# Moving one low-part subtraction to GpSimd and the gate's activation ahead of it, at the turn from gate/up to down in the wide experts

## The chip, the core and the metric

One core of a Trainium2 chip runs the whole block: TensorE (PE, with its weight loads PEld), VectorE (DVE), ScalarE (ACT), GpSimd (POOL) and SyncE (SP), which issues most weight loads. The metric is the device time of one launch in microseconds (us).

## The reference, cut to what matters

The block is a gated MLP mixer and a gated delta net, then a mixture of 32 experts, four for each of 512 tokens. The change lies in the expert's middle:

```python
gu = xb @ w_gu[e] + b_gu[e]
gate = jnp.minimum(gu[:, :D_FF], SWIGLU_LIMIT)
up = jnp.clip(gu[:, D_FF:], -SWIGLU_LIMIT, SWIGLU_LIMIT)
act = gate * jax.nn.sigmoid(SWIGLU_ALPHA * gate) * (up + 1)
return (act @ w_down[e] + b_down[e]) * wt[:, None]
```

`w_gu` is 1024 x 2048 and `w_down` 1024 x 1024 for each expert, all in float32.

## The kernel before, in words

Experts are sorted by their number of tokens and each sits at a fixed place p, 0 to 31, in the program; `CAPS[RANKS[p]]` is the number of rows that the place can hold. Eight places hold 128 rows or more and are called wide here: p = 3, 9, 17 and 29 hold 128; p = 5, 13, 21 and 25 hold 192 or 160, that is a `Wide` unit of 128 rows and a second `Unit` of 64 or 32. The other 24 places are narrow and use plain float32 matmuls.

A wide place computes with float32r matmuls in three passes: weights and activations are split into a high part (`hi`, a copy rounded to float32r) and a low part (`lo`, the difference). `split_w` makes both for one 128 x 1024 piece of weights: the high part is a copy on ACT (L1410, `whi`), the low part a subtraction on DVE (L1411, `wlo`). Three pairs of buffers go round (`N_PAIRS = 3`). A place has 16 such pieces for gate/up and 8 for down, and the pair of the second down piece was last used by the gate/up piece next to last.

`run(p, ...)` is one place: the gate/up matmuls over eight chunks of weights, then the turn, then the down matmuls over eight pieces f. In the turn of a wide place each half c (512 columns) goes through `swiglu`: on ACT a relu and a sigmoid of the gate (L1423, L1424), on DVE the clipped up part `u` (L1425), the product with the gate `r` (L1426) and `u = (u + 1) * r` (L1427), where both inputs are SBUF tiles of `f16` (in the trace they are called f). PE transposes each half (L1549), ACT copies it as the high part `ath` (L1551) and DVE subtracts for the low part `atl` (L1552). `between` transposes the next place's rows on PE, and `behind` modulates them on ACT and DVE.

From here on every engine's order is that of the code (a manual schedule). The weights pass through a ring of 14 chunks of 1 MB: SP loads a chunk ahead as soon as PE, or the split, has read the slot. On GpSimd's queue only gathers (L1302) and the adding scatters of finished rows (L1764) run in this stage; in the first 320 us, GpSimd has made low parts of other weights (L158) with the same kind of instruction.

Of the kernel before, what the change touches and what calls it, by code (L numbers as in the profile page):

```python
# [6 lines left out]
F32 = mybir.dt.float32  # L7
# [5 lines left out]
OP = mybir.AluOpType  # L13
# [43 lines left out]
def hybrid_block(tc, x, c, w_ada, b_ada, norm1_w, w_in, gm_vnorm_w, gm_w_spatial, gm_b_spatial,  # L57
# [3 lines left out]
    V, S, G, T = nc.vector, nc.scalar, nc.gpsimd, nc.tensor  # L61
# [110 lines left out]
    ready = []  # L172
# [11 lines left out]
    def take():  # L184
        ahead(3)
        n_used[0] += 1
        return ready[n_used[0] - 1]
# [66 lines left out]
    for f in range(3):  # L254
        w = take()
# [42 lines left out]
    for n in range(5):  # L298
        V.tensor_scalar(ta[:, 0, :], ta[:, 2, :], n, 1, op0=OP.logical_shift_right,
                        op1=OP.bitwise_or)  # L300
# [383 lines left out]
    for f in range(3):  # L684
        w = take()
# [81 lines left out]
    for n in range(4):  # L767
        p1s = []
        for gs in halves:
            p1 = bank([P, 8, 32])  # L770
            p1s.append(p1)
            for c8 in range(8):
                for q in range(4):
                    r = slice(q * 32, q * 32 + 32)
# [5 lines left out]
        for gs in halves:  # L780
            p2 = bank([P, 8, 32])
            p2s.append(p2)
            for c8 in range(8):
                for q in range(4):
                    r = slice(q * 32, q * 32 + 32)
# [37 lines left out]
    for g in range(4):  # L823
        gs = slice(g * 4, g * 4 + 4)
        kk = bank([P, 4, 2, CH])
        for c4 in range(4):
            ch, hp = divmod(g * 4 + c4, 2)
            for hb in range(2):
                r = slice(hb * 64, hb * 64 + 64)
# [23 lines left out]
    for g in range(2):  # L853
        for hb in range(2):
            r = slice(hb * 64, hb * 64 + 64)
# [142 lines left out]
    w = [take() for _ in range(4)]  # L998
# [45 lines left out]
    def load_chunk(i):  # L1044

        p, j = divmod(i, 12)
        if p < NE:
            load_part(ring[i % N_RING], bass.ds(ids[p], 1) if p else slice(0, 1), j)

    def load_id(p):  # L1050
        if p >= NE or not p:
            return
        ids[p] = nc.values_load(eids[0:1, p:p + 1], engines=[mybir.EngineType.SP], min_val=0, max_val=NE - 1,
                                skip_runtime_bounds_check_because="a permutation of the experts")

    op = ExitStack()
# [117 lines left out]
    both = range(2)  # L1174
# [83 lines left out]
    act_tiles = [f16[:, 2 + i // 2, (i % 2) * 512:(i % 2) * 512 + 512] for i in range(4)]  # L1258
# [142 lines left out]
                part.turn()  # L1401
                part.modulate()

    def split_w(w):

        i = n_split[0] % N_PAIRS
        n_split[0] += 1
        hi = xp.tile([P, D], F32R, name="whi", tag=f"x2_{2 * i}") if i < 2 else mp.tile([P, D], F32R, name="whi", bufs=1)
        lo = xp.tile([P, D], F32R, name="wlo", tag=f"x2_{2 * i + 1}") if i < 2 else mp.tile([P, D], F32R, name="wlo", bufs=1)
        S.activation(hi, w, AF.Copy)  # L1410
        V.tensor_tensor(lo, w, hi.bitcast(F32), op=OP.subtract)  # L1411
        return hi, lo

    n_split = [0]
# [2 lines left out]

        return ((h[0], w[0]), (h[1], w[0]), (h[0], w[1]))

    def swiglu(gate, up, r, u):  # L1420

        n = gate.shape[0]
        S.activation(r, gate, AF.Relu, scale=-1.0, bias=sevens[0:n, 0:1])  # L1423
        S.activation(r, r, AF.Sigmoid, scale=-1.702, bias=sevens[0:n, 1:2])  # L1424
        V.tensor_scalar(u, up, 7.0, -7.0, op0=OP.min, op1=OP.max)  # L1425
        V.scalar_tensor_tensor(r, gate, 7.0, r, op0=OP.min, op1=OP.mult)  # L1426
        V.scalar_tensor_tensor(u, u, 1.0, r, op0=OP.add, op1=OP.mult)  # L1427
        return u

    class Unit:  # L1430
# [43 lines left out]
        def act(self):  # L1474
            i = (0, 1) if not self.second else (0, 2) if self.part.first else (2, 3)
            r, u = (act_tiles[j][:, 0:self.w] for j in i)
            self.a = swiglu(self.gate, self.up, r, u)
# [40 lines left out]
    class Wide:  # L1518


        n, w, ng, off, second, banks = P, D, 1, 0, False, 5
# [17 lines left out]
                    mm(self.gu[c * 2 + q], l[:, k, :], r[:, q * 512:q * 512 + 512], False, k == KC - 1 and i == 2)  # L1539

        def act(self):
            self.a = [swiglu(self.gu[c], self.gu[2 + c], act_tiles[2 * c], act_tiles[2 * c + 1]) for c in both]

        def turn(self):
            self.at, self.al = (mp.tile([P, KC, P], F32R, name=nm, bufs=1) for nm in ("ath", "atl"))
# [200 lines left out]
    def last_rows(u):  # L1746

        y_last, junk, rest, same, factor, nf_u = (last_tiles[nm] for nm in ("y_last", "junk", "rest", "same", "factor", "nf_u"))
        y, s_ = y_last[:, 0:u.w], ssn[:, NT:NT + 1]
        V.tensor_tensor(y, u.dn, factor[:, 0:u.w], op=OP.mult)  # L1750
        V.tensor_tensor(y, y, rest[:, 0:u.w], op=OP.add)  # L1751
        V.scalar_tensor_tensor(junk[:, 0:u.w], y, 1.0, y, op0=OP.mult, op1=OP.mult, accum_out=s_)  # L1752
        ps = psT2.tile([P, 512], F32, name="t")[:, 0:1]
        mm(ps, same, s_)
        norm(s_, ps)
        V.scalar_tensor_tensor(y, y, s_, nf_u[:, 0:u.w], op0=OP.mult, op1=OP.mult)  # L1756
        G.indirect_dma_start(out=u.rows(out[0]), out_offset=bass.IndirectOffsetOnAxis(ap=u.idx, axis=0), in_=y,  # L1757
                             in_offset=None, bounds_check=SEQ * D // u.w - 1, oob_is_err=False)

    def add_rows(u):  # L1760

        y = mp.tile([P, 512 if u.second else D], F32, name="yx" if u.second else "yo", bufs=1)[:, 0:u.w]
        u.weighted(y)
        G.indirect_dma_start(out=u.rows(acc), out_offset=bass.IndirectOffsetOnAxis(ap=u.idx, axis=0),  # L1764
                             in_=y, in_offset=None, compute_op=OP.add,
                             bounds_check=SEQ * D // u.w - 1, oob_is_err=False)

    def run(p, side, between, behind):

        units = place[p].units
        w = [ring[(p * 12 + j) % N_RING] for j in range(12)]
        load_id(p + 3)
        for u in units:
            u.gu_start()
        split = place[p].split
        for k in range(KC):
            if split:
                for c in both:  # L1780
                    units[0].gu_parts(k, c, split_w(w[k][:, c * D:(c + 1) * D]))
            for u in units[split:]:
                u.gu_chunk(k, w[k])
            load_chunk(p * 12 + k + N_RING)
            side(k)

        def source(f):
            return w[KC + f // 2][:, (f % 2) * D:(f % 2) * D + D]

        ready = [split_w(source(0))] if split else []  # L1790
        for u in units:
            u.act()
        between()
        room = sum(u.banks for u in units) + len(units) < 6
        for u in units if room else ():
            u.down_start()
        for u in units:
            u.turn()
        for u in () if room else units:
            u.down_start()  # L1800
        if split:
            ready += [split_w(source(1)), split_w(source(2))]
        for f in range(KC):
            behind(f)
            if split:
                units[0].down_parts(f, ready.pop(0) if ready else split_w(source(f)))
            for u in units[split:]:
                u.down_chunk(f, source(f))
            if f % 2:
                load_chunk(p * 12 + KC + f // 2 + N_RING)  # L1810
        for u in units:
            last_rows(u) if p == NE - 1 else add_rows(u)
# [11 lines left out]
    def side(p):  # L1824
        def at(k):
            if k == 0:
                hots(p + 2)
            elif k == 1 and not late(p):
                find(p + 2)
            elif k == 2 and not late(p):  # L1830
                spread(p + 2)

        return at

    def between(p):
        def at():
            if p == 0:
                for _ in steps:
                    pass
                spread(2)  # L1840
            place[p + 1].turn()
            if p and late(p):
                find(p + 2)

        return at

    def behind(p):
        def at(f):
            if f == 0:
                place[p + 1].parts[0].modulate()  # L1850
            elif f == 4:
                place[p + 1].more_turn()
                if p + 2 < NE:
                    if p and late(p):
                        spread(p + 2)
                    place[p + 2].gather()

        return at

    run(0, side_0, between(0), behind(0))  # L1860
    for p in range(1, NE - 1):
        run(p, side(p), between(p), behind(p))
    run(NE - 1, lambda k: early(k, place[NE - 1].units[0]), lambda: None, early_norms)


# [80 lines left out]
```

## Time and profile before

| | us |
|---|---|
| median of three runs (lowest, highest) | 1528.15 (1523.21, 1534.48) |
| profiled execution | 1526.17 |
| its span, first to last instruction | 1524.4 |
| PE busy | 1401.4 (92%) |
| DVE busy | 694.7 (46%) |
| ACT busy | 475.7 (31%) |
| GpSimd busy | 237.0 (16%) |

Matmuls are pipelined, so a busy PE need not be at its peak, and busy time at a granted clock of one half counts like any other. Shares are averages: the expert stage lies from about 364 us to 1507 us.

### The profile page before, as it was taken

The page shows a single profiled execution, that of the slowest core. Times are in us where ns is not written, and L with a number is a line of the kernel's source. Part 1 is how long each engine was busy: PE and PEld are TensorE (multiplying, and loading weights), DVE is VectorE, ACT ScalarE, POOL GpSimd, SP SyncE. Part 2 cuts the span into 40 slices and gives each one's busy share as a digit, 9 for nine tenths or more (in the row PEclk, how much of TensorE's full clock was granted, in tenths as well). Part 3 has the DMA queues.
Part 4 walks back from the last instruction along what each step waited for, and adds up shares of the span by engine and source line. Part 5 has one row for each costly group of instructions (what it writes and reads, how often), then busy time and mean ns, then how long its engine had stood idle before and what let it go on. Part 6 is the DMA issues. An engine that isn't in the chain of part 4 may idle for free. (4 is left out here: it accounts for less than half of the span.)

```text
span 1524.4 us, 23439 instructions
## 1 busy us (share of the span) xinstructions
PE 1401.4 (92%) x9161; PEld 737.2 (48%) x9161; DVE 694.7 (46%) x1352; ACT 475.7 (31%) x735; POOL 237.0 (16%) x218
## 2 busy tenths in 40 slices
PE   4898999998899999999999999999999999999982
PEld 3555897775337454246334523642454235424621
DVE  4674628984229453147115512831462146214713
ACT  4343332321127242135015411711351135113501
POOL 2243433530011100110010011000101010101010
PEclk9999999998999999999999999999999999999995
DMA  9566331168699996999999699999978997899973
GB/s 326 180 240 212 99 117 47 59 249 354 240 404 410 401 398 205 407 396 407 395 407 408 230 370 406 404 391 409 399 309 317 410 387 264 308 411 396 390 295 119
DMA packets 113698, 479.35 MB, mean 314 GB/s; under 512 B 15172, under 2 KB 28649, under 8 KB 80811
## 3 DMA queue, kind: packets, MB, share of 16 engines
q1 hardware_dynamic: 98176, 454.10, 76.2%
q0 software_dynamic: 10096, 18.87, 5.1%
q10 hardware_dynamic: 5306, 4.80, 1.0%
q8 instruction: 74, 1.21, 0.3%
q14 instruction: 46, 0.37, 0.1%
HBM read 466.21 MB, written 17.96 MB: 318 GB/s over the span
## 5 line engine op out<-in xcount | busy, mean ns | idle before, releaser
L71 PE MATMUL gu<-ring,h 128*64 128x512 f32 (+1 forms) x1984 | 381.1, 599 | 0.0
L1411 DVE TENSOR_TENSOR wlo<-ring,whi 128x1024 fp32r<-128x1024 f32 x192 | 229.2, 1222 | 48.8 <-ACT whi L1410 47.8
L71 PE MATMUL gu<-ring,at 128*32 128x256 f32 (+1 forms) x1536 | 237.4, 508 | 13.9 <-ACT at L1485 13.9
L1410 ACT ACTIVATE whi<-ring 128x1024 fp32r<-128x1024 f32 x192 | 200.7, 1060 | 115.0 <-PE gu L71 92.1
L71 PEld LDWEIGHTS gu<-ring,h 128*64 128x64 f32 (+1 forms) x1984 | 104.8, 128 | 245.0 <-issue 232.0
L1423 ACT ACTIVATE f<-gu,sevens 128x512 f32<-128x512 f32 (+1 forms) x51 | 32.1, 630 | 529.7 <-PE gu L71 527.5
L1425 DVE TENSOR_SCALAR f<-gu 128x512 f32<-128x512 f32 (+1 forms) x51 | 31.7, 622 | 298.1 <-PE gu L71 280.5
L71 PEld LDWEIGHTS gu<-ring,at 128*32 128x32 f32 (+1 forms) x1536 | 64.7, 125 | 164.7 <-issue 129.7
L1302 POOL DMA_INDIRECT f<-xnd,idx x35 | 36.0, 1028 | 537.4 <-PE gu L1483 277.4
L1764 POOL DMA_INDIRECT acc<-yo,idx x31 | 55.9, 1802 | 401.5 <-DVE yo L1505 238.0
L158 POOL TENSOR_TENSOR wlo<-w,whi 128x1024 fp32r<-128x1024 f32 x32 | 80.8, 2530 | 138.2 <-ACT whi L157 135.9
L71 PE MATMUL gu<-whi,hh 128*128 128x512 f32 x256 | 84.1, 410 | 0.0
L71 PE MATMUL gu<-wlo,hh 128*128 128x512 f32 x256 | 80.8, 397 | 0.8 <-DVE wlo L1411 0.4
L71 PE MATMUL gu<-whi,hl 128*128 128x512 f32 x256 | 80.1, 394 | 0.0
L1505 DVE SCALAR_TENSOR_TENSOR yo<-gu,info,g2x 128x512 f32<-128x512 f32 (+1 forms) x23 | 16.5, 716 | 130.4 <-PE gu L71 130.4
L71 PEld LDWEIGHTS gu<-whi,hh 128*128 128x128 f32 x256 | 45.6, 188 | 33.1 <-ACT whi L1410 18.2
L71 PEld LDWEIGHTS gu<-wlo,hh 128*128 128x128 f32 x256 | 47.6, 188 | 13.8 <-DVE wlo L1411 3.2
L71 PEld LDWEIGHTS gu<-whi,hl 128*128 128x128 f32 x256 | 48.1, 188 | 11.2
L71 PE MATMUL bank<-hhi,whi 128*128 128x512 f32 x160 | 50.2, 432 | 1.9 <-ACT hhi L247 1.8
L71 PE MATMUL gu<-whi,ath 128*128 128x512 f32 x128 | 49.4, 470 | 0.0
L1483 PE MATMUL gu<-ident,f 128*128 128x128 f32 x114 | 19.9, 299 | 31.3 <-DVE f L1427 30.9
L71 PE MATMUL gu<-wlo,ath 128*128 128x512 f32 x128 | 44.0, 427 | 4.9 <-DVE wlo L1411 4.9
(435 smaller groups left out, 1761.7 us busy)
## 6 DMA issues: line engine op xcount, KB each, us to landing
ring<-in_w_gu_dram SPq DMA_DIRECT2D x256, 1024.0 KB, 16.8
ring<-in_w_down_dram SPq DMA_DIRECT2D x128, 1024.0 KB, 19.1
adaw<-in_w_ada_dram SPq DMA_DIRECT2D x32, 512.0 KB, 4.9
w<-in_w_in_dram SPq DMA_DIRECT2D x24, 512.0 KB, 3.7
ada<-in_w_ada_dram SPq DMA_DIRECT2D x16, 512.0 KB, 10.1
w<-in_w_out_dram SPq DMA_DIRECT2D x8, 512.0 KB, 3.4
x<-in_x_dram SPq DMA_DIRECT2D x4, 512.0 KB
x<-in_x_dram ACTq DMA_DIRECT2D x4, 512.0 KB
```

Of the source, the lines that this page charges most:

```text
L71: T.matmul(o, l, r, start=start, stop=stop, skip_group_check=True)
L158: G.tensor_tensor(lo, w, hi.bitcast(F32), op=OP.subtract)
L1302: G.indirect_dma_start(out=self.xg, out_offset=None, in_=xnd[:, :], in_offset=bass.IndirectOffsetOnAxis(ap=self.from_[0:self.n], axis=0), ...
L1410: S.activation(hi, w, AF.Copy)
L1411: V.tensor_tensor(lo, w, hi.bitcast(F32), op=OP.subtract)
L1423: S.activation(r, gate, AF.Relu, scale=-1.0, bias=sevens[0:n, 0:1])
L1425: V.tensor_scalar(u, up, 7.0, -7.0, op0=OP.min, op1=OP.max)
L1483: T.transpose(t[:, j, :], self.a[:, j * P:(j + 1) * P], ident)
L1505: V.scalar_tensor_tensor(y, self.dn, self.wt, g2x[self.n], op0=OP.mult, op1=OP.mult)
L1764: G.indirect_dma_start(out=u.rows(acc), out_offset=bass.IndirectOffsetOnAxis(ap=u.idx, axis=0), in_=y, in_offset=None, compute_op=OP.add, ...
```

## The change

`split_w` takes the engine of the subtraction. In a wide place, both halves' relu and sigmoid are now issued on ACT right behind the first down piece's split, and behind them the second down piece's split, whose high part comes on ACT ahead of the turned activations' copies and whose low part is made on GpSimd instead of DVE. In the wide unit DVE takes the gate's product `r` ahead of the clipped `u`. The third down piece stays where it was. Narrow units keep their order. The rows on PE and SP are the same in the two programs, in the same order.

```diff
-    def split_w(w):
+    def split_w(w, engine=V):
...
         S.activation(hi, w, AF.Copy)
-        V.tensor_tensor(lo, w, hi.bitcast(F32), op=OP.subtract)
+        engine.tensor_tensor(lo, w, hi.bitcast(F32), op=OP.subtract)
         return hi, lo
...
-    def swiglu(gate, up, r, u):
-
+    def gate_side(gate, r):
         n = gate.shape[0]
         S.activation(r, gate, AF.Relu, scale=-1.0, bias=sevens[0:n, 0:1])
         S.activation(r, r, AF.Sigmoid, scale=-1.702, bias=sevens[0:n, 1:2])
-        V.tensor_scalar(u, up, 7.0, -7.0, op0=OP.min, op1=OP.max)
-        V.scalar_tensor_tensor(r, gate, 7.0, r, op0=OP.min, op1=OP.mult)
+
+    def swiglu(gate, up, r, u, started=False):
+
+        if started:
+            V.scalar_tensor_tensor(r, gate, 7.0, r, op0=OP.min, op1=OP.mult)
+            V.tensor_scalar(u, up, 7.0, -7.0, op0=OP.min, op1=OP.max)
+        else:
+            gate_side(gate, r)
+            V.tensor_scalar(u, up, 7.0, -7.0, op0=OP.min, op1=OP.max)
+            V.scalar_tensor_tensor(r, gate, 7.0, r, op0=OP.min, op1=OP.mult)
         V.scalar_tensor_tensor(u, u, 1.0, r, op0=OP.add, op1=OP.mult)
         return u
...
-            self.a = [swiglu(self.gu[c], self.gu[2 + c], act_tiles[2 * c], act_tiles[2 * c + 1]) for c in both]
+            self.a = [swiglu(self.gu[c], self.gu[2 + c], act_tiles[2 * c], act_tiles[2 * c + 1], True) for c in both]
...
         ready = [split_w(source(0))] if split else []
+        if split:
+            for c in both:
+                gate_side(units[0].gu[c], act_tiles[2 * c])
+            ready.append(split_w(source(1), G))
         for u in units:
             u.act()
         between()
...
         if split:
-            ready += [split_w(source(1)), split_w(source(2))]
+            ready.append(split_w(source(2)))
```

ACT in the turn of place 9, before (L1423 relu, L1424 sigmoid, L1551 the high part of the turned activations, L1410 high parts of weights; ring_3368 holds the first two down pieces, ring_3369 the next two):

```order
L1410 ACTIVATE whi<-ring_3368 128x1024
L1423 ACTIVATE f_3800<-gu,sevens 128x512
L1424 ACTIVATE f_3800<-f_3800,sevens 128x512
L1423 ACTIVATE f_3800<-gu,sevens 128x512
L1424 ACTIVATE f_3800<-f_3800,sevens 128x512
L1551 ACTIVATE ath<-gu 128x512 x2
L1410 ACTIVATE whi<-ring_3368 128x1024
L1410 ACTIVATE whi<-ring_3369 128x1024
L1345 ACTIVATE h<-t,sh_502,s_503 128x64 x4
```

ACT in the same turn, after the change:

```order
L1410 ACTIVATE whi<-ring_3368 128x1024
L1422 ACTIVATE f_3800<-gu,sevens 128x512
L1423 ACTIVATE f_3800<-f_3800,sevens 128x512
L1422 ACTIVATE f_3800<-gu,sevens 128x512
L1423 ACTIVATE f_3800<-f_3800,sevens 128x512
L1410 ACTIVATE whi<-ring_3368 128x1024
L1558 ACTIVATE ath<-gu 128x512 x2
L1410 ACTIVATE whi<-ring_3369 128x1024
L1345 ACTIVATE h<-t,sh_502,s_503 128x64 x4
```

The second piece's copy has moved ahead of the two `ath` copies; in a place of one unit the relus and sigmoids stand where they stood.

DVE in that turn, before:

```order
L1425 TENSOR_SCALAR f_3800<-gu 128x512
L1426 SCALAR_TENSOR_TENSOR f_3800<-gu,f_3800 128x512
L1427 SCALAR_TENSOR_TENSOR f_3800<-f_3800 128x512
L1425 TENSOR_SCALAR f_3800<-gu 128x512
L1426 SCALAR_TENSOR_TENSOR f_3800<-gu,f_3800 128x512
L1427 SCALAR_TENSOR_TENSOR f_3800<-f_3800 128x512
L1294 COPY info<-t 96x2
L1296 TENSOR_SCALAR idx<-info 96x1
L1552 TENSOR_TENSOR atl<-gu,ath 128x512 x2
L1411 TENSOR_TENSOR wlo<-ring_3368,whi 128x1024
L1411 TENSOR_TENSOR wlo<-ring_3369,whi 128x1024
```

DVE in that turn, after (L1428 is `r`, L1429 `u`, L1434 their product):

```order
L1428 SCALAR_TENSOR_TENSOR f_3800<-gu,f_3800 128x512
L1429 TENSOR_SCALAR f_3800<-gu 128x512
L1434 SCALAR_TENSOR_TENSOR f_3800<-f_3800 128x512
L1428 SCALAR_TENSOR_TENSOR f_3800<-gu,f_3800 128x512
L1429 TENSOR_SCALAR f_3800<-gu 128x512
L1434 SCALAR_TENSOR_TENSOR f_3800<-f_3800 128x512
L1294 COPY info<-t 96x2
L1296 TENSOR_SCALAR idx<-info 96x1
L1559 TENSOR_TENSOR atl<-gu,ath 128x512 x2
L1411 TENSOR_TENSOR wlo<-ring_3369,whi 128x1024
```

The first two instructions of each half have changed places, and the subtraction of ring_3368 is gone from DVE.

GpSimd around that turn, after; before, the same queue without the L1411 row:

```order
L1302 DMA f_3800<-xnd,idx 64x1024
L1771 DMA acc<-yo,idx 1024x512
L1411 TENSOR_TENSOR wlo<-ring_3368,whi 128x1024
L1302 DMA f_3800<-xnd,idx 96x1024
L1771 DMA acc<-yo,idx 512x1024
```

The subtraction stands between the scatter of place 8 and the gather for place 11.

## Rows read from the trace of the kernel before

**Rows 1.** The page's first part: busy time and share of each engine.
```profile
PE 1401.4 (92%) x9161; PEld 737.2 (48%) x9161; DVE 694.7 (46%) x1352; ACT 475.7 (31%) x735; POOL 237.0 (16%) x218
```

**Rows 2.** Waits of PE's matmuls, 399 to 1500 us: total, times, longest.
```profile
PE gu L71 <- DVE wlo L1411: 5.4, 7, 0.8
PE gu L1549 <- DVE info L1294: 4.8, 4, 1.3
PE gu L1549 <- DVE f L1427: 4.2, 6, 0.9
```

**Rows 3.** The same view of PE's weight loads and of SP.
```profile
PEld gu L71 <- DMA ring<-in_w_gu_dram: 14.3, 30, 0.8
...
SPq L1038 <- PE gu L71: 301.9, 169, 4.6
```

**Rows 4.** Windows: a stretch of gate/up matmuls in narrow place 2.
```profile
431.00:446.00 15.00, 15.00 (x78) 5.64 (x73) 1.11 (x5) 1.32 (x2) 1.83 (x2) 1.00 1.02 403
```

**Rows 5.** Timeline of the turn in place 9: start, duration, engine, instruction.
```profile
699.75 0.63 PE L71 MATMUL gu<-wlo,hh 128*128 128x512 f32 x2
...
700.84 0.72 ACT L1424 ACTIVATE f<-f,sevens 128x512 f32<-128x512 f32 x1
...
701.50 0.69 DVE L1427 SCALAR_TENSOR_TENSOR f<-f 128x512 f32<-128x512 f32 x1
...
702.34 0.63 PE L1549 MATMUL gu<-ident,f 128*128 128x128 f32 x4 [0.56 <-DVE f L1427]
702.71 0.68 DVE L1426 SCALAR_TENSOR_TENSOR f<-gu,f 128x512 f32<-128x512 f32 x1
...
703.43 0.69 DVE L1427 SCALAR_TENSOR_TENSOR f<-f 128x512 f32<-128x512 f32 x1
...
704.27 0.63 PE L1549 MATMUL gu<-ident,f 128*128 128x128 f32 x4 [1.30 <-DVE info L1294]
...
704.98 1.33 PE L71 MATMUL gu<-whi,ath 128*128 128x512 f32 x2
705.18 1.02 POOL L1302 DMA_INDIRECT f<-xnd,idx  x1 [25.04 <-PE gu L1549]
705.43 2.00 ACT L1410 ACTIVATE whi<-ring 128x1024 fp32r<-128x1024 f32 x2
...
706.51 2.36 DVE L1411 TENSOR_TENSOR wlo<-ring,whi 128x1024 fp32r<-128x1024 f32 x2 [0.25 <-ACT whi L1410]
...
707.82 0.93 PE L71 MATMUL gu<-whi,ath 128*128 128x512 f32 x2
```

**Rows 6.** Timeline of the turn in place 13, which has a second unit.
```profile
849.48 0.72 ACT L1424 ACTIVATE f<-f,sevens 128x512 f32<-128x512 f32 x1
...
852.06 0.69 DVE L1427 SCALAR_TENSOR_TENSOR f<-f 128x512 f32<-128x512 f32 x1
```

**Rows 7.** Timeline of an early stretch in which GpSimd makes a low part.
```profile
288.39 1.05 ACT L157 ACTIVATE whi<-w 128x1024 fp32r<-128x1024 f32 x1
...
289.52 2.50 POOL L158 TENSOR_TENSOR wlo<-w,whi 128x1024 fp32r<-128x1024 f32 x1 [4.68 <-ACT whi L157]
289.70 0.41 DVE L954 TENSOR_TENSOR vk<-bank,nrm 128x256 f32<-128x256 f32 x1
...
290.37 2.20 DVE L569 TENSOR_TENSOR yy<-yy,gu 128x512 f32<-128x512 f32 x1
```

**Rows 8.** Timeline of another early stretch, with a scalar-tensor-tensor on DVE.
```profile
236.30 2.36 POOL L154 TENSOR_TENSOR w<-w,g1row 128x1024 f32<-128x1024 f32 x1 [3.44 <-DMA w<-in_w_out_dram]
236.32 2.37 DVE L86 SCALAR_TENSOR_TENSOR rs<-ry 128x4 f32<-128x4 f32 x1
```

**Rows 9.** Durations by line, shortest/median/longest in ns, first and last start.
```profile
L569 DVE TENSOR_TENSOR yy<-yy,gu x4: 684/1994/2196, 264.1 to 290.4; 128x512 f32<-128x512 f32 x4
...
L158 POOL TENSOR_TENSOR wlo<-w,whi x32: 2338/2398/3259, 23.8 to 313.6; 128x1024 fp32r<-128x1024 f32 x32
```

**Rows 10.** Windows of place 9 behind the turn: busy by engine, then granted clock.
```profile
705.00:708.40 3.40, 3.40 (x10) 2.63 (x9) 2.58 (x3) 3.40 (x7) 1.02 (x1) 0.51 1.00 417
```

## The prediction

> **What bounds the kernel now.** I read the page's first part for the engines, then who PE waits for in the expert stage, then the turn of one wide place in order of time, and last the early stretch in which GpSimd did what it is now asked to do. PE is busy for 92% of the span, DVE for 46%, ACT for 31% and GpSimd for 16% [rows 1]. It is not DMA that holds PE: its weight loads waited for the ring 14.3 us in 30 pieces of at most 0.8 us, while SP waited for PE to free slots for 301.9 us [rows 3]. A narrow place shows the same: 15.0 us of gate/up matmuls without a gap at the full clock [rows 4]. So a microsecond by which the turn of a wide place is longer or shorter on PE is one on the whole, and eight places have such a turn.
>
> Look now at the turn of place 9 [rows 5]. The last gate/up pair starts on PE at 699.75. ACT ends the second half's sigmoid at 700.84 + 0.72 = 701.56. DVE goes through six instructions one behind the other; the last, the second half's product of `u` and `r`, starts at 703.43 and ends at 704.12. PE transposes that half at 704.27 and starts the down matmuls at 704.98. The reader is to see that the chain which keeps PE waiting here is DVE's six, and that the second and third pieces' splits, on ACT at 705.43 and on DVE at 706.51, come behind it. PE takes the second piece's first pass at 707.82, after it was ready. PE's matmuls waited for weights' low parts 5.4 us in the whole expert stage [rows 2].
>
> **The change, part by part.** *The second piece's subtraction leaves DVE.* It took 2.36 / 2 = 1.18 us in each turn [rows 5], 9.4 us in eight. It lay behind the chain, beside PE's first down passes, so I count nothing. What its removal could win is bounded by all the waits for low parts, 5.4 us [rows 2]; those I saw lie later in the down stage, where buffers and copies for the next places hold the split, and the same pieces stay there.
>
> *The second piece's copy on ACT moves ahead of the `ath` copies.* ACT is free from 701.56 until PE has transposed the first half (702.34 + 0.63 = 702.97) [rows 5]. The copy takes about 1.05 us; two back to back took 2.00 [rows 5], so it can start 0.1 us before the sigmoid's end and is over at about 702.52. The first `ath` copy isn't held up in a place of one unit. With a second unit the relu of that unit starts some tenths later, and DVE wants it only behind the wide unit's six. Zero. If that cover were gone, it would cost at most the copy, 1.05 us.
>
> *DVE takes `r` ahead of `u`.* The same six instructions; the first can begin when the first sigmoid is done instead of when the up half is done, which are within 0.1 us of each other. Zero, 0.1 us a place at most either way.
>
> *The subtraction on GpSimd.* When ACT's copy was over, GpSimd began 289.52 - (288.39 + 1.05) = 0.08 us later [rows 7]. So it begins at about 702.60 here. Its queue is free: before the change it sat idle for 25.04 us ahead of the gather at 705.18 [rows 5]. Undisturbed it takes 2.40 us, the median of 32 such [rows 9], and ends at 705.00. Nothing waits for its result until PE's second piece, past 707.8. By that alone it would be free.
>
> But look at what DVE did in the early stretch while GpSimd worked. With GpSimd's subtraction from 289.52 to 292.02, DVE's `vk` at 289.70, one of whose inputs is in PSUM (a bank), took 0.41 us; `yy` at 290.37, which reads two SBUF tiles, took 2.20 us and ended at 292.57, 0.55 us after GpSimd [rows 7]. Undisturbed, the same line takes 0.684 us [rows 9]. The scalar-tensor-tensor on two SBUF tiles at 236.32, tiny as it is, lasts 2.37 us and ends with GpSimd's instruction at 236.30 + 2.36 [rows 8]. I found eight DVE instructions of 128x512 on two SBUF tiles that began while such a GpSimd instruction ran: all eight ended 0.55 us behind its end (the last one is the one in rows 7), and none with a PSUM input was stretched.
>
> Now the product that ends the chain, `u = (u + 1) * r`, reads two SBUF tiles. It wants to start at 703.43, and GpSimd is busy from 702.60 to 705.00. It would then end at 705.00 + 0.55 = 705.55 instead of 704.12: **1.43 us later**. Queued behind it on DVE are the copies of the next places' numbers and both `atl` subtractions (and, with a second unit, that unit's three instructions); PE waits for it to transpose, ACT for PE, and the down matmuls for all of them. The other five of the six read a PSUM bank, or (the first half's product, 701.50 to 702.19) are over before GpSimd begins. In place 13 the sigmoid ends at 850.20 and the product at 852.75 [rows 6], 2.55 us apart against 704.12 - 701.56 = 2.56 in place 9: the same geometry, so the same 1.43 us. The sum is 8 x 1.43 = 11.4 us.
>
> Bounds: with GpSimd's shortest, 2.338 us [rows 9], it is 1.37 us a place and 11.0; with its longest, 3.259, it is 2.29 and 18.3. I take the median, since the long ones began while DVE held two SBUF tiles, and at 702.60 DVE is in an instruction with a PSUM input (the one at 702.71 or the one ahead of it) [rows 5].
>
> A rule speaks to this. The Trainium skill's page SBUF — State Buffer, section SBUF: two separate sides, says that DVE, with two SBUF inputs, and GpSimd, when it reads SBUF, take turns whole instruction by whole instruction, whichever began first, and the other blocks entirely; the trace agrees, with the eight. The page GPSIMD Engine Reference, section 3.1, gives some 2.6 cycles an element for a two-input instruction, at 1.2 GHz. An estimate from that page is 1024 x 2.6 / 1.2 = 2.2 us instead of the measured 2.40; by it the sum would be 8 x 1.25 = 10 us.
>
> *The clock.* Behind the turn PE is at half speed for a while: from 705.00 to 708.40 the granted clock is 0.51, that is 1.2 GHz instead of 2.4 [rows 10], and a pair of down matmuls takes 1.33 us where a gate/up pair took 0.63 [rows 5]. With PE starting 1.43 us later, up to 1.43 us of that half-clock stretch falls into waiting instead of work, which gives back 0.7 us; the transposes, at 704.27 still fast (0.63 us), fall into it and lose up to 0.6; and a second such stretch may follow. I take zero, with bounds of -0.7 and +1.7 us (half of 3.4) a place.
>
> So the profiled execution, 1526.2 us (span 1524.4 and 1.8 around it), would become 1537.6. The median of the three runs, 1528.15, is 2.0 us above it; the forecast goes by the median: 1528.15 + 11.4 = **1539.5 us**.
>
> **The rivals.** *A second half-clock stretch in each turn.* The wait on PE grows by half again, and a stretch of 3.4 us at half speed gives 1.7 us more a place: 8 x (1.43 + 1.7) = 25 us, 1553. For it: the clock fell in the turn of every wide place, behind a wait. Against it: where the stretch falls varies from place to place, and the later start of PE saves part of it. The skill's page TensorE: Matmul & The Clock Gate, section on HAM oscillation, says that a wait long enough lets the clock fall anew each time; the trace agrees in that the clock falls at the turn [rows 10], and no run here yet shows a longer wait.
>
> *DVE's product comes first: not slower.* If GpSimd begins after 703.43 in place 9, that is over 0.83 us later than worked out, the product runs as before and GpSimd is the one that waits, with time to spare until 707.8. Then nothing is lost: 1528. The point from which it decides is GpSimd's start against the product's. For it: the copy on ACT or GpSimd's wait for several semaphores might be slower than in rows 7. Against it: 0.08 us is what rows 7 show, and GpSimd's queue is empty then.
>
> *The split was the bound after all.* If the waits for low parts went away, 5.4 us come back and GpSimd costs nothing: 1523. Against it: in rows 5 the second piece is ready before PE wants it.
>
> **How the numbers follow.** A measurement of this kernel can tell about 1% (15.3 us) from no change: its three runs alone lie 11 us apart. I give the forecast 0.62, the second half-clock stretch 0.20, DVE first 0.13 and the split as bound 0.05. The range is to leave out no more than two in ten: 1530 shuts out the last two for the most part (0.15 or so), 1552 takes in the clock in most of its places, and the bounds 11.0 and 18.3 lie inside. The threshold for slower by over 1% is 1543.4. The forecast, 3.9 us below it, passes it about once in seven (0.09), the clock mostly (0.17): 0.26. Faster by over 1% needs 1512.9, which no case reaches: 0.02. Within 1%: 0.72.
>
> **What would show it.** In the profile after, the product in a wide turn (L1434) should last about 2.1 us instead of 0.69 for the second half, end 0.55 us behind GpSimd's L1411, and PE's transposes of the second half should start some 1.4 us later against the sigmoid's end; GpSimd's eight new instructions should take 2.4 us each. The first half's product should stay at 0.69. If the product keeps 0.69 us and starts ahead of GpSimd, the second rival holds; if PE's half-clock stretches double in number, the first. The prediction is wrong if the turn is longer by under 1 us, or if other places change.

## The result and the profile after

The changed kernel takes 1549.02 us, the median of six launches, against 1527.72 for six of the kernel before; the ratio is 1.0131, 95% interval 1.0097 to 1.0165. (One of the six took 4596 us, which is not explained; ratios here and below leave out a launch that took over 1.5% more than the fastest of its kernel, that is this one and two of x1. The other five lie between 1544.24 and 1551.29.) The profiled execution took 1548.65 us, with a span of 1546.8, against 1526.17 and 1524.4. The time is inside the range of 1530 to 1552, 9.5 us above the forecast of 1539.5: the loss is nearly twice the predicted 11.4 us.

The page's head, the line on engines, and the group of the new GpSimd instruction and of the product, by source line (shortest/median/longest in ns, first to last start):

```profile
span 1546.8 us, 23458 instructions
PE 1410.9 (91%) x9161; PEld 743.5 (48%) x9161; DVE 699.6 (45%) x1344; ACT 475.8 (31%) x735; POOL 253.6 (16%) x226
...
L1434 DVE SCALAR_TENSOR_TENSOR f<-f x51: 424/692/2030, 403.1 to 1515.4; 128x512 f32<-128x512 f32 x38, 128x256 f32<-128x256 f32 x13
L1411 POOL TENSOR_TENSOR wlo<-ring,whi x8: 2336/2345/2349, 485.8 to 1446.9; 128x1024 fp32r<-128x1024 f32 x8
```

DVE has eight instructions fewer (1344 against 1352) and is busy longer (699.6 us against 694.7): eight subtractions of about 1.2 us are gone (9.7 us), and each second product of a wide turn, like the one below, lasts some 2.0 us instead of 0.69 (10.6 us in all). Of the difference 2.3 us lie ahead of the expert stage, which the change doesn't touch. PE, with the same 9161 matmuls, is busy 9.5 us longer [rows 1]: more of its work has been done at a lower clock. Its waits in the expert stage (399 to 1525 us; total, times, longest):

```profile
PE gu L1556 <- DVE f L1434: 10.2, 7, 2.4
PE gu L1556 <- DVE info L1294: 10.1, 4, 2.6
PE gu L71 <- DVE wlo L1411: 5.3, 7, 0.8
```

The transposes' two waits grew from 4.8 + 4.2 = 9.0 us to 10.2 + 10.1 = 20.3, by 11.3 us, while the wait for low parts stayed (5.4 and 5.3) [rows 2]. The `info` named as releaser is only what DVE did right behind the product. The turn of place 9, in order of time (start, duration, engine, instruction):

```profile
707.67 0.72 ACT L1423 ACTIVATE f<-f,sevens 128x512 f32<-128x512 f32 x1
...
708.30 1.04 ACT L1410 ACTIVATE whi<-ring 128x1024 fp32r<-128x1024 f32 x1
708.42 0.69 DVE L1434 SCALAR_TENSOR_TENSOR f<-f 128x512 f32<-128x512 f32 x1
...
709.26 0.63 PE L1556 MATMUL gu<-ident,f 128*128 128x128 f32 x4 [0.65 <-DVE f L1434]
709.48 2.34 POOL L1411 TENSOR_TENSOR wlo<-ring,whi 128x1024 fp32r<-128x1024 f32 x1 [22.52 <-ACT whi L1410]
...
710.35 2.02 DVE L1434 SCALAR_TENSOR_TENSOR f<-f 128x512 f32<-128x512 f32 x1
...
712.51 1.08 PE L1556 MATMUL gu<-ident,f 128*128 128x128 f32 x4 [2.62 <-DVE info L1294]
...
713.39 1.06 PE L71 MATMUL gu<-b,sel_o 96*128 96x512 bf16 x2
...
713.88 1.41 PE L71 MATMUL gu<-whi,ath 128*128 128x512 f32 x2
```

Held against [rows 5], the first half's product still takes 0.69 us. GpSimd runs from 709.48 to 711.82; the second half's product begins inside that and ends at 710.35 + 2.02 = 712.37, 0.55 us behind GpSimd. Between the two halves' transposes lie 712.51 - 709.26 = 3.25 us, where there were 704.27 - 702.34 = 1.93: PE starts 1.32 us later. Over the eight turns this distance grew by 1.32 to 1.44 us, 11.1 in all, and all eight products ended 0.55 us behind GpSimd. The second transposes themselves now take 1.08 us, not 0.63. The windows around that turn (stretch, length, busy time of PE, PEld, DVE, ACT and POOL, then the granted clock as a share of the full one, DMA share, GB/s) say why:

```profile
709.20:712.00 2.80, 0.63 (x4) 0.42 (x4) 2.77 (x3) 0.74 (x2) 2.34 (x1) 0.98 1.01 421
712.00:718.80 6.80, 6.29 (x17) 4.90 (x18) 5.12 (x9) 3.67 (x8) 1.03 (x1) 0.51 1.01 410
718.80:722.00 3.20, 3.20 (x15) 2.30 (x13) 0.00 (x0) 2.52 (x3) 0.00 (x0) 1.00 1.01 348
683.50:729.40 45.90, 41.71 (x180) 32.10 (x178) 36.54 (x42) 27.86 (x32) 5.65 (x3) 0.93 1.02 408
```

PE is at 0.51 (1.2 GHz) for 6.8 us behind the turn, where before it was for 3.4 [rows 10]. The last row is the whole of place 9; before, it was 43.20 us at a clock of 0.96:

```profile
676.70:719.90 43.20, 40.42 (x182) 31.17 (x180) 36.30 (x43) 27.73 (x32) 3.31 (x2) 0.96 1.02 407
```

Of the 2.70 us that place 9 lost, 1.32 are the wait. The extra 3.4 us at half speed cost up to 1.7, and a little comes back where waiting, not work, falls into the stretch.

**The sum over the places.** The table cuts each profile into places, from a place's first bias matmul (`gu<-b,sel_o`) to that of the next, and adds up in us, for the eight wide places and the narrow ones from place 1 to 30, the time and the part of it at a granted clock of one half (called half clock from here on). All of it is worked out from one profiled launch of each kernel; the last column is what all launches gave, x1 to x5 and f1 to g2 being the experiments below.

| kernel | wide places | of it at half clock | narrow places | of it at half clock | ratio to before, 95% |
|---|---|---|---|---|---|
| before | 418.1 | 34.1 | 634.1 | 17.1 | 1 |
| after | 435.5 | 51.2 | 636.6 | 23.9 | 1.0131 (1.0097 to 1.0165) |
| x1_low_on_dve | 419.9 | 37.5 | 629.0 | 6.8 | 0.9998 (0.9970 to 1.0025) |
| x2_pool_halves | 421.2 | 37.5 | 630.6 | 10.2 | 1.0024 (0.9999 to 1.0050) |
| x3_up_in_psum | 417.3 | 30.7 | 641.4 | 34.1 | 1.0031 (0.9997 to 1.0064) |
| x4_delay_by_hand | 433.3 | 51.2 | 636.6 | 23.9 | 1.0082 (1.0049 to 1.0115) |
| x5_pool_late | 422.3 | 41.0 | 629.3 | 6.8 | 1.0006 (0.9988 to 1.0023) |
| f1_fill_2_6 | 408.6 | 3.4 | 642.4 | 37.5 | 0.9999 (0.9976 to 1.0021) |
| f2_fill_3_9 | 415.2 | 3.4 | 633.6 | 17.1 | 0.9997 (0.9973 to 1.0022) |
| f3_changed_fill_2_12 | 417.5 | 3.4 | 633.9 | 17.1 | 0.9999 (0.9974 to 1.0024) |
| g1_fill_all | 408.5 | 3.4 | 635.2 | 10.2 | 0.9944 (0.9912 to 0.9975) |
| g2_fill_narrow | 419.6 | 37.5 | 634.8 | 10.2 | 1.0044 (1.0015 to 1.0074) |

Of the 22.4 us by which the two spans differ, 17.4 lie in the wide places: half of 51.2 - 34.1 = 17.1 us is 8.6 us of clock, and 8.8 are left for the waits. The five wide places with a second stretch grew by 2.6 to 2.8 us each, the three without (3, 17 and 25) by 0.8 to 1.8. The launches say about the same. Each comes with its time and its mean granted clock, and 2 x (1 - clock) x time is its time at half clock. Half of that is what it cost, as an estimate from above, since a part falls into waits. Before: a mean of 1528.5 us over the 35 launches measured beside f1, f2, f3 and x5, with 121.9 us at half clock, so 1528.5 - 61.0 = 1467.6 without that cost. After: 1548.0 over five, 144.3 and 1475.9. So the 19.5 us between them are some 8.3 of waiting and (144.3 - 121.9) / 2 = 11.2 of clock.

### The profile page after: what moved, and what is told of

The parts are those of the page before. It is cut to its first block, busy times and chain, and to the rows that moved or that the text cites. A ratio compares the mean times of both kernels' runs of the same rounds, so it can differ in the third digit from the quotient of the medians.

```text
span 1546.8 us, 23458 instructions
## 1 busy us (share of the span) xinstructions
PE 1410.9 (91%) x9161; PEld 743.5 (48%) x9161; DVE 699.6 (45%) x1344; ACT 475.8 (31%) x735; POOL 253.6 (16%) x226
## 5 line engine op out<-in xcount | busy, mean ns | idle before, releaser
L1411 DVE TENSOR_TENSOR wlo<-ring,whi 128x1024 fp32r<-128x1024 f32 x184 | 220.4, 1223 | 55.9 <-ACT whi L1410 54.6
L1410 ACT ACTIVATE whi<-ring 128x1024 fp32r<-128x1024 f32 x192 | 201.7, 1060 | 125.1 <-PE gu L71 98.7
L1432 DVE TENSOR_SCALAR f<-gu 128x512 f32<-128x512 f32 (+1 forms) x35 | 20.7, 591 | 287.3 <-PE gu L71 269.7
L1411 POOL TENSOR_TENSOR wlo<-ring,whi 128x1024 fp32r<-128x1024 f32 x8 | 18.8, 2344 | 221.1 <-ACT whi L1410 198.5
L71 PEld LDWEIGHTS gu<-whi,hl 128*128 128x128 f32 x256 | 48.1, 188 | 11.2
## 6 DMA issues: line engine op xcount, KB each, us to landing
ada<-in_w_ada_dram SPq DMA_DIRECT2D x16, 512.0 KB, 10.2
```

What stands on the lines that cost most here:

```text
L71: T.matmul(o, l, r, start=start, stop=stop, skip_group_check=True)
L1411: engine.tensor_tensor(lo, w, hi.bitcast(F32), op=OP.subtract)
```

## The experiments

Two theories stand against each other at first. By the first, GpSimd's subtraction blocks the product of two SBUF tiles, and that wait, with what it does to PE's clock, is the whole loss. By its rivals, ACT's copy that was moved ahead, the new order of `r` and `u`, or the loss of the old subtraction's place is part of it. The second question is how much the clock adds, and whether it belongs to the wait or to GpSimd. "x" kernels edit the change or imitate it, "f" and "g" kernels give PE idle work in its waits.

**x1: the low part back on DVE, all else of the change kept.** The copy on ACT stays ahead; DVE subtracts at the old place.

```diff
-            ready.append(split_w(source(1), G))
+            ready.append(split_w(source(1), None))    # the high part alone
...
+            V.tensor_tensor(ready[1][1], source(1), ready[1][0].bitcast(F32), op=OP.subtract)
             ready.append(split_w(source(2)))
```

> The gate side, the order of r and u and the second piece's copy on ACT stay as changed; only its low part goes back to DVE, behind the atl subtractions. If GpSimd's subtraction blocks the product on two SBUF tiles (the theory), the second half's product lasts 0.69 us again, PE's second transposes start 1.9 us behind its first in place 9 (changed kernel: 3.25), and the time is that of the kernel before, 1528 (ratio 0.997 to 1.004). If the new order on ACT or on DVE is what costs (the rival), it stays near 1549 (ratio 1.013).

Measured: 1530.45 us against 1528.35, ratio 0.9998. The turn of place 9:

```profile
708.36 0.63 PE L1557 MATMUL gu<-ident,f 128*128 128x128 f32 x4 [0.65 <-DVE f L1435]
...
709.45 0.69 DVE L1435 SCALAR_TENSOR_TENSOR f<-f 128x512 f32<-128x512 f32 x1
...
710.29 0.63 PE L1557 MATMUL gu<-ident,f 128*128 128x128 f32 x4 [1.30 <-DVE info L1294]
```

The product is back at 0.69 us, the transposes are 1.93 us apart, and the second ones run at full clock. The loss goes with the subtraction on GpSimd; the earlier copy and the swapped `r` and `u` cost nothing that can be measured (the interval of the ratio is 0.9970 to 1.0025, some 4 us either way).

**x2: the same subtraction in two GpSimd instructions of 512 columns.**

```diff
-        engine.tensor_tensor(lo, w, hi.bitcast(F32), op=OP.subtract)
+        for cs in (slice(0, 512), slice(512, D)) if engine is G else (slice(0, D),):
+            engine.tensor_tensor(lo[:, cs], w[:, cs], hi[:, cs].bitcast(F32), op=OP.subtract)
```

> The changed kernel with GpSimd's subtraction cut into two instructions of 512 columns, same work, same place. The theory, with waiting by whole instruction: the first half takes about 1.2 us and ends some 0.3 us after the product wants to start, the product slips in before the second half and ends about 0.3 us later than in the kernel before, so the turn is longer by 0.2 to 0.4 us instead of 1.33 and the time is 1529 to 1534. If the second half gets ahead of the waiting product, or if the cost is the order or GpSimd's presence as such, 1545 to 1550.

Measured: 1533.82 us, ratio 1.0024. In place 9:

```profile
703.26 0.63 PE L1557 MATMUL gu<-ident,f 128*128 128x128 f32 x4 [0.65 <-DVE f L1435]
703.48 2.94 POOL L1412 TENSOR_TENSOR wlo<-ring,whi 128x512 fp32r<-128x512 f32 x2 [22.54 <-ACT whi L1410]
704.35 0.95 DVE L1435 SCALAR_TENSOR_TENSOR f<-f 128x512 f32<-128x512 f32 x1
...
705.44 1.01 PE L1557 MATMUL gu<-ident,f 128*128 128x128 f32 x4 [1.56 <-DVE info L1294]
```

The product waits for the first half alone, 0.95 us instead of 2.02, and the second GpSimd instruction then waits for it: the pair spans 2.94 us instead of 2.34. The transposes are 2.18 us apart, 0.25 more than before. All eight turns show it (0.90 to 0.95 us). So GpSimd holds the product up for one instruction, and a waiting DVE instruction gets in between two of GpSimd's.

**x3: the clipped up part kept in PSUM.** GpSimd's work is untouched; the product reads one SBUF tile and one bank instead of two SBUF tiles.

```diff
-            V.tensor_scalar(u, up, 7.0, -7.0, op0=OP.min, op1=OP.max)
+            V.tensor_scalar(up, up, 7.0, -7.0, op0=OP.min, op1=OP.max)
...
-        V.scalar_tensor_tensor(u, u, 1.0, r, op0=OP.add, op1=OP.mult)
+        V.scalar_tensor_tensor(u, up, 1.0, r, op0=OP.add, op1=OP.mult)
```

> The changed kernel with the clipped up part left in its PSUM bank, so that the product in a wide unit reads one PSUM and one SBUF tile; GpSimd's subtraction stays where it is. The theory: the product takes 0.7 us while GpSimd works, the turn is that of the kernel before, 1526 to 1530. If GpSimd's work in the turn costs through anything else than two SBUF inputs, 1545 to 1550.

```profile
702.56 0.63 PE L1558 MATMUL gu<-ident,f 128*128 128x128 f32 x4 [0.65 <-DVE f L1430]
702.77 2.35 POOL L1411 TENSOR_TENSOR wlo<-ring,whi 128x1024 fp32r<-128x1024 f32 x1 [22.52 <-ACT whi L1410]
...
703.65 0.69 DVE L1430 SCALAR_TENSOR_TENSOR f<-gu,f 128x512 f32<-128x512 f32 x1
...
704.49 0.77 PE L1558 MATMUL gu<-ident,f 128*128 128x128 f32 x4 [1.30 <-DVE info L1294]
```

In the middle of GpSimd's 2.35 us the product takes 0.69, and the transposes are 1.93 us apart, as before the change. For this product it is the second SBUF input that is blocked, not DVE as such. The Trainium skill's page SBUF — State Buffer, section SBUF: two separate sides, has the rule of the turns; this run agrees, and shows for the product itself what [rows 7] showed for other lines. The median, 1537.93 us, was a miss all the same. In the profiled launch (1532.56 us) the wide places take 417.3 us, 0.8 less than before; the excess is in the narrow ones, which this edit doesn't touch and where half-clock time doubled to 34.1 us. Over its launches (1522 to 1543) time less half the half-clock time is 1467.5, as before (1467.6). The mechanism held, the kernel was not faster for it.

**x4: the kernel before, with the wait made by hand.** Two extra clips on DVE, which write the same values once more, ahead of the second half's product. GpSimd does nothing.

```diff
+        for m in more:                      # (512, 512) in the second half, else ()
+            V.tensor_scalar(u[:, 0:m], up[:, 0:m], 7.0, -7.0, op0=OP.min, op1=OP.max)
         V.scalar_tensor_tensor(u, u, 1.0, r, op0=OP.add, op1=OP.mult)
```

> The kernel before, with two more copies of the clip instruction on DVE ahead of the second half's product (idle repeats of what stands there): the chain is 1.2 us longer in each wide turn and GpSimd does nothing. If a delay of the chain is all that the change costs, directly (8 x 1.22 = 9.8 us) and through more half-clock time on PE behind it (about 0.8 us a turn in the changed kernel, so 6 us), the time is 1540 to 1547 (ratio 1.008 to 1.013), with half-clock stretches in wide places up from 10. If the clock has no part in it, 1537 to 1538.

Measured: 1541.11 us, the median of six, ratio 1.0082. The profiled launch was the slowest of the six, 1555.22 us; of the 29.0 us by which its span is longer than before, 11.3 lie ahead of place 1 (which starts at 427.4 us, before at 416.1), where the edit changes nothing, and 17.7 in the places of the table. In place 9, and the windows behind it:

```profile
718.40 0.63 PE L1552 MATMUL gu<-ident,f 128*128 128x128 f32 x4 [0.56 <-DVE f L1429]
...
719.36 1.41 DVE L1428 TENSOR_SCALAR f<-gu 128x512 f32<-128x512 f32 x2
...
720.80 0.69 DVE L1429 SCALAR_TENSOR_TENSOR f<-f 128x512 f32<-128x512 f32 x1
721.64 1.08 PE L1552 MATMUL gu<-ident,f 128*128 128x128 f32 x4 [2.62 <-DVE info L1294]
```
```profile
721.00:727.80 6.80, 6.16 (x17) 4.77 (x18) 5.43 (x10) 4.62 (x8) 1.02 (x1) 0.50 1.02 413
```

The transposes are 3.24 us apart, as in the changed kernel, with the same second stretch at half clock. The wide places take 433.3 us with 51.2 of them at half clock; the changed kernel has 435.5 and 51.2. So the wait brings the clock's share with it, without GpSimd. By the launches x4 costs 12.5 us (7.5 to 17.6) and the changed kernel 20.0 (14.8 to 25.2). The intervals overlap, so a few us of the 20 that come from something besides the wait are not excluded.

**f3: the changed kernel, with PE kept at work in the wait.** Idle matmuls, whose sums are overwritten by the transposes, stand ahead of the first half's (2) and the second half's (12) in the wide turn. f1 and f2 are the same edit on the kernel before, with 2 and 6, 3 and 9.

```diff
                 t = psG.tile([P, 4, P], F32, name="gu")
+                for _ in range((2, 12)[c]):
+                    mm(t.rearrange("p a b -> p (a b)"), self.h[0][:, 0, :], self.h[1][:, 0:4, :])
                 for j in range(4):
```

> The changed kernel, with two idle matmuls ahead of the first half's transposes and twelve ahead of the second's (2.6 us, about what PE waits there with GpSimd in the way). If of the changed kernel's 20 us some 10.6 are the wait itself (8 x 1.33) and the rest the clock, this takes away the clock's part and more: 1528 + 10.6 - 10 = 1526 to 1533, well under the changed kernel's 1549 although the product is blocked as before (it lasts 2.0 us in the profile). If the clock has no part, 1545 to 1550.

Measured: 1528.17 us against 1528.10, ratio 0.9999.

```profile
706.50 2.38 POOL L1411 TENSOR_TENSOR wlo<-ring,whi 128x1024 fp32r<-128x1024 f32 x1 [22.52 <-ACT whi L1410]
706.61 3.05 PE L71 MATMUL gu<-hl,hh 128*128 128x512 f32 x12
...
707.37 2.07 DVE L1434 SCALAR_TENSOR_TENSOR f<-f 128x512 f32<-128x512 f32 x1
...
709.49 0.66 PE L1558 MATMUL gu<-ident,f 128*128 128x128 f32 x4
...
710.23 0.81 PE L71 MATMUL gu<-whi,ath 128*128 128x512 f32 x2
```
```profile
703.60:712.00 8.40, 8.40 (x50) 6.38 (x49) 6.99 (x11) 5.14 (x9) 3.41 (x2) 1.00 1.01 420
```

The product is as blocked as ever (2.07 us), yet the clock is 1.00 through the turn and the first down pair takes 0.81 us where it took 1.41. The wide places are back at 417.5 us, with 3.4 at half clock instead of 51.2. All of the change's 20 us is gone without its wait being gone: PE works at full speed behind the wait, which pays for it. Held against f1 below, where the kernel before has the like help, the wait still costs 417.5 - 408.6 = 8.9 us in the wide places, what the sum above had left for it (8.8).

**f1 and f2: the kernel before, with the same fill.**

> The kernel before, with PE kept at work in the wide turn: two idle matmuls of 512 columns ahead of the first half's transposes and six ahead of the second's, into the bank that the transposes then overwrite (their results are used by nobody). They take 0.21 us each at the full clock, 0.4 and 1.3 us, about what PE waits there. If the waiting is what lowers the granted clock, the half-clock stretches in wide places (10 in the profile before, some 1.5 us each) go for the most part and the time falls by 8 to 14 us, to 1514 to 1520 (ratio 0.991 to 0.995). If the clock falls whatever PE does there, the idle matmuls run at half speed in part and hold up the transposes: 1528 to 1535.

> As the run with two and six, with three and nine idle matmuls: 0.6 us a turn more on PE than it waits, 5 us in eight. If two and six don't keep the clock up and this does, it is the faster of the two by up to 8 us; if two and six suffice, it is the slower by about 5 us.

Measured: 1527.07 and 1525.84 us, ratios 0.9999 and 0.9997: no gain, where f1 was expected to win 8 to 14 us. In f1 the whole of place 9 shows what was hoped for, 42.20 us at a clock of 1.00:

```profile
683.10:725.30 42.20, 41.21 (x188) 31.00 (x186) 36.23 (x43) 26.69 (x31) 3.31 (x2) 1.00 1.02 404
```

The wide places fell by 9.5 us to 408.6, but the narrow ones rose by 8.3, with half-clock time going from 17.1 to 37.5. In f2 the fill is longer than the wait, and the wide places keep only 2.9 us of it.

**x5: GpSimd's subtraction late.** The copy goes back behind the `ath` copies, so that the product is out of its way.

```diff
-            ready.append(split_w(source(1), G))
...
-            ready.append(split_w(source(2)))
+            ready += [split_w(source(1), G), split_w(source(2))]
```

> The second piece's low part on GpSimd, but with its copy on ACT back at the old place behind the ath copies; the gate side and the order of r and u as changed. The theory: GpSimd begins at about 4.2 us behind PE's first transposes in place 9, when the chain of six is over, and now meets DVE's subtraction for the third piece, also on two SBUF tiles, which ends some 1.2 us later than in the kernel before, just about when PE wants it; 0 to 0.5 us a turn, 1527 to 1533. If GpSimd is too slow for the second piece wherever it starts, 1540 and more.

Measured: 1530.61 us, ratio 1.0006.

```profile
708.92 2.39 POOL L1411 TENSOR_TENSOR wlo<-ring,whi 128x1024 fp32r<-128x1024 f32 x1 [26.55 <-ACT whi L1410]
709.76 2.63 DVE L1411 TENSOR_TENSOR wlo<-ring,whi 128x1024 fp32r<-128x1024 f32 x1 [1.20 <-ACT whi L1410]
```

The product is free, and the blocked one is now DVE's third piece, which ends at 712.39, 1.08 us behind GpSimd's 711.31. PE waits no longer for that piece (5.3 us for low parts in all, as before). So GpSimd takes 1.2 us of DVE's work here and makes DVE wait 1.4 us.

**g1 and g2: fills in the narrow places too.** Four idle matmuls ahead of the first unit's transposes in each narrow place, on top of f1 (g1) and alone (g2).

```diff
+            if not self.second:
+                wide_sel = (sel_o[:, p:p + 1] if p else sel[:, 0:1]).to_broadcast([96, P])
+                for _ in range(4):
+                    mm(t4.rearrange("p a b -> p (a b)"), wide_sel, b3[:, 0:512])
```

> The kernel before with idle matmuls in the turns of all places: two and six in the wide ones as in the run f1, and four of 512 columns in bfloat16 (nobody uses their results) ahead of the first unit's transposes in each narrow place, where PE waits some 0.8 us for the product. In f1 the wide places lost nearly all their half-clock time (3.4 us left of 34.1) and were 9.5 us shorter together, but the narrow places showed 37.5 us of it instead of 17.1 and took it back. If the waiting in the narrow turns is what lowers the clock there, it goes as well: half-clock time over the whole span from 113 to some 75 us, and the time 1508 to 1518, below both kernels. If four are too few or the clock falls in narrow places for another reason, 1524 to 1532.

> The four idle matmuls in narrow places alone, none in the wide ones. If the two work each by itself, this takes away the narrow places' half-clock time (17 us in the profile before, 7 to 9 us of time) and leaves the wide ones': 1519 to 1525. If four idle matmuls don't hold the clock in narrow places, 1528 to 1534, since they are then only some 0.1 to 0.3 us a place too long.

Measured: g1 1521.82 us against 1529.02, ratio 0.9944 (0.9912 to 0.9975), which beats the kernel before, if by less than the 1508 to 1518 hoped for; g2 1535.45, ratio 1.0044 (1.0015 to 1.0074), a miss. The turn of narrow place 10 in g1, where the first row holds two bias matmuls and the four idle ones:

```profile
741.99 1.38 PE L71 MATMUL gu<-b,sel_o 96*64 96x512 bf16 x6
743.39 0.66 PE L1489 MATMUL gu<-ident,f 128*128 128x128 f32 x4
```

Over the launches g1 spends 85.8 us at half clock (before: 125.6 on the same chip), and g2 124.2. The narrow fills alone give back nothing, and their own work shows: g2's time less half its half-clock time is 1474.1, some 6 us more than before. They pay only where the wide turns are filled as well.

## Why the prediction was right in kind and short in size

**The blocked product** came as predicted: GpSimd at 709.48, 0.14 us behind ACT's copy (0.08 had been read from [rows 7]); the end 0.55 us behind GpSimd, as in those rows; the first half's product untouched. x3 shows the cause by the second SBUF input and x1 that nothing else in the change costs anything. The predicted 1.43 us is 1.32 in place 9 (GpSimd takes 2.34 us, not the median of 2.40 in [rows 9] but next to its shortest, and starts 0.04 us earlier against the first transposes), and up to 1.44 in others. Eight turns give 11.1 us of 11.4.

**The step that failed** is the clock: "I take zero, with bounds of -0.7 and +1.7 us (half of 3.4) a place". It measured 8.6 us in the wide places of the profile, 1.1 a place, and 11.2 over the launches. Both ends had their reason, and the choice of the middle between them had none. The two parts that were to offset each other came as described: in place 9 the stretch at half clock begins 2.62 us behind the first transposes (2.73 before), so 0.6 us of it now fall into the wait, and the second transposes fall into the rest and take 1.08 us instead of 0.63. What the sum had at nothing is that the stretch goes on: five turns have 6.8 us where they had 3.4, so that there are 15 stretches of 3.4 us in the wide places instead of 10. The rival that held this let the wait grow "by half again"; with the predicted delay the wait ahead of the second transposes goes from 1.30 us [rows 5] to 2.73, over twice as long (2.62 measured). The Trainium skill's page TensorE: Matmul & The Clock Gate, section HAM oscillation, tells of a clock that falls anew behind every wait that is long enough, in a kernel that waits for DMA. That the waits of this turn are long enough x4 and f3 show, since the wait without GpSimd brings the same 51.2 us at half clock and GpSimd's wait with PE at work brings 3.4. The time lies inside the range because its upper end was drawn for the clock in most places, not because the sum was right.

**The rivals.** The second stretch, given 0.20 and 1553, was nearer (1549.0) than the forecast: it happened in five of the eight places; places 3 and 25 had two stretches before already, and place 17 kept one. That DVE's product comes first did not happen: GpSimd began 0.87 us ahead of it. The split was not the bound: waits for low parts are 5.3 us as they were 5.4. The loss was over 1%, which had been given 0.26, and it came by way of that one rival.

**What stays open.** Why narrow places take back half-clock time when wide ones lose it (f1, x3), and don't with their own turns filled as well (g1), isn't settled. Their code is the same in f1 as before, their start against the end of the last stretch is not. The reading that it is the moment of a narrow turn's wait that decides would need runs that shift it alone, which weren't made. Nor does every fall of the clock come behind a wait, as the prediction has it. In place 3 of the kernel before it falls at 483.20 us, ahead of that turn's one wait, 0.88 us; up to there PE was at work, at the last on matmuls of two columns and on transposes:

```profile
480.89 1.95 PE L71 MATMUL t<-tw,pm 128*128 128x2 f32 x16
482.70 0.64 PE L1549 MATMUL gu<-ident,f 128*128 128x128 f32 x4
484.22 1.09 PE L1549 MATMUL gu<-ident,f 128*128 128x128 f32 x4 [0.88 <-DVE info L1294]
```
```profile
483.20:490.00 6.80, 5.92 (x18) 4.55 (x17) 5.73 (x14) 5.21 (x9) 2.03 (x2) 0.50 1.01 417
```

The 3.4 us that f1, f2, f3 and g1 keep in the wide places all lie there. What lets the clock fall in that turn isn't shown.

## What to carry to other kernels

An idle GpSimd is no free engine as long as the critical chain has a DVE step with two SBUF inputs beside it: give that step a PSUM input (x3), start GpSimd behind it (x5), or cut GpSimd's instruction so that DVE gets in between (x2). Each of the three removed the loss or most of it, and none was faster than the kernel before (1.0006 to 1.0031). Where the profile shows the clock already falling in a turn, price a longer wait there at more than its length: 11.1 us of waits cost 20 us here, and 10.6 cost 12.5 in x4. And look at the time at half clock as a cost of its own: idle matmuls in every wait that lets the clock fall took 0.6% off the kernel before (g1), while filling one kind of turn alone took off nothing.

## What the runs showed of the hardware that was not expected

- Time less half the half-clock time is nearly constant for one kernel: over 35 launches of the kernel before it is 1467.6 us with a standard deviation of about 1.7, while the times themselves range over 17 us (1521.5 to 1538.4); over 23 on another chip it is 1468.3 with 3.1, over a range of 20 us. So launches of this kernel differ for the most part by how long the clock was at one half.
- A blocked DVE instruction has most of its work still to do when GpSimd's ends: the product of 128x512, 0.69 us long, ends 0.55 us behind it, the subtraction of 128x1024, 1.22 us long, 1.08 us behind it (all eight of x5).
- Two SBUF inputs are not the only case. In the early stage of the kernel before, a cast from one SBUF tile to another (L889, 96x512) that began at 184.50 us, 0.04 us behind a GpSimd subtraction, took 2.62 us where three others take 0.41, and ended 0.28 us behind GpSimd. Casts of 32x512 (L894) at 190.47 us ran at 0.41 beside one, which itself took 3.11 us. Which one-input steps are blocked isn't shown.
- Idle matmuls in the wait held the granted clock at 1.00 through the turn (f3, 703.60 to 712.00), and doing more on PE made the changed kernel end earlier (1528.17 us instead of 1549.02).
